# When TensorE's part of the gate tables is traced: at the step that makes its operands, or at the next weight

## The chip, the cores and the metric

The kernel runs on one core of a Trainium2 chip. The engines are TensorE (PE: matmuls, with PEld for its weight loads), VectorE (DVE), ScalarE (ACT), GpSimd (POOL, which issues the gathers here) and SyncE (SP, which issues the other DMAs). Each engine takes its instructions in a fixed order and waits where an operand or a buffer isn't ready. The metric is the time of one execution on the device in microseconds (us), as a median of several runs.

## What is computed

One block of a hybrid encoder over 1024 tokens of width 1024, in float32: a state space branch and a convolution branch, merged; then a mixer that looks up experts (PEER); then an embedding gate and a norm. The change touches the mixer alone:

```
scores = einsum("thcd,hckd->thck", q, keys)         # 8 heads, 2 halves, 128 keys each
sv, si = top_k(scores, 16)
best, j = top_k(all 16 x 16 sums of the two halves, 16)
expert = i1 * 128 + i2                              # one of 16384
gate = softmax(best)
act = gelu(einsum("thkd,td->thk", u_tab[expert], x))
out = einsum("thk,thkd->td", gate * act, v_tab[expert])
```

So each token has 8 x 16 = 128 chosen experts, each with a row of u_tab, a row of v_tab and a gate.

## The kernel before

The tokens are worked in two halves h of 512, each in four blocks b of 128. The mixer treats its blocks in two ways.

*Gathered blocks* (b of 0 and 1, four in all). `gather_up` fetches, for one choice of 128 tokens at a time, the rows of u_tab by an indirect DMA on POOL (L767) and multiplies and sums them with the tokens on DVE (L786). `gather_down` fetches rows of v_tab, four at a time, and PE adds them up with eight column-tiled matmuls ("gv", L814). All fetched rows lie in one ring of eight buffers, "row".

*Dense blocks* (b of 2 and 3). All 16384 experts are run: `dense_up(e)` takes the e-th 128 rows of u_tab, transposed (128 such blocks), as a weight, multiplies it with the 512 dense tokens and applies gelu. The result z goes to DRAM (DZ) or on to `dense_down`, which multiplies it by the table of gates (DG, zero where an expert wasn't chosen) and by v_tab's rows. One dense unit is 24 matmuls of 128x512, since every operand is split into a rounded part and a rest (`mm3`: L178, L179, L181).

`gate_table(i)` builds the table of one dense block i. First `choose_block` has found the choices; PE transposes them (L716) and ACT copies them to kt and wt. Then, for 4 tokens at a time (a *step*, 32 steps to a table in four chunks of eight), DVE makes the one-hot rows of both key numbers (L738) and puts the gates into the second (L740); PE multiplies the two (four products of 128x128, L744) and ACT copies the result to four tiles S (L747), which are written to DG at the end of a chunk (L750). The one-hots, too, lie in the "row" ring.

What sets the order: `weight()` loads a 128x1024 weight, splits it on ACT (L161) and DVE (L162), and then calls `tick`, which hands out work that lies beside the dense matmuls. Each tick adds a credit to three queues of generators (cq, gq, rq), and each is run until its yields have used the credit; a yield of None ends that turn. In the stage "up", gq holds a weave of the choices and tables (one after the other) with the gathers of u, one step of each in turn, and rq holds `gather_down`. What the generators trace is placed behind the tick's subtract (`issue_after`). A scheduler then fixes the order on each engine. Stage "up" runs dense units until gq is empty and the count is a multiple of four: 92 units. The rest of the 128 blocks come in "both" (up and down together, 36 blocks), and "down" then takes the 92 stored ones.

## Time and profile before

| | us |
|---|---|
| median of 3 runs | 4184.51 (4184.32 to 4186.64) |
| the profiled execution | 4184.43 |
| its span, first to last instruction | 4182.6 |
| stage "up" in the span | about 2020 to 2980 |
| stage "both" | about 2980 to 3394 |
| stage "down" | about 3394 to 4010 |

All times in the rows further below count from the start of the span. PE's busy time is that of pipelined matmuls; the granted clock is the share of 2.4 GHz that PE was given. A wait names the engine whose instruction could start only later, its line, what released it, the sum in us, how often, and the longest.

### The profile page before, as it was taken

Reading aid. Unit: us, or ns where it says so; the run is one execution under the profiler, and the core shown is the slowest. Engines: PE = TensorE matmul, PEld = TensorE weight load, DVE = VectorE, ACT = ScalarE, POOL = GpSimd, SP = SyncE. Lnnn points to the kernel's source line nnn. Section 1 sums busy time; section 2 is a strip of 40 time slices with the busy share of each in tenths; the row PEclk is TensorE's granted clock in tenths of the full one; section 3 lists DMA queues with packets and bytes.
Section 4 is the critical chain, followed back from the end, with each engine's and each line's share of the span. In section 5 each row is a group of like instructions: output and inputs, shape, how many; then the busy total and the mean of one; then the engine's idle time right before and its main releaser. Section 6 shows DMA issues by size and latency. Waiting matters only on the chain.

```text
span 4182.6 us, 51212 instructions
## 1 busy us (share of the span) xinstructions
PE 3783.2 (90%) x17800; PEld 2861.6 (68%) x17800; DVE 3121.7 (75%) x5907; ACT 1497.7 (36%) x2626; POOL 1283.1 (31%) x1087
## 2 busy tenths in 40 slices
PE   8999998899988897999879787888999999999987
PEld 6887776677866665667557565666777767777766
DVE  7889888989987876768978677677665656755545
ACT  4135565443345553433223232323322212222243
POOL 0000000000232433544655544454355444422000
PEclk9999998999999998999889898889999999999998
DMA  4243333453676878998989888888999999988632
GB/s 147 87 160 108 98 109 125 139 169 114 246 246 202 291 272 308 345 358 316 332 297 354 307 318 325 307 314 332 334 340 348 320 336 372 335 303 296 210 113 81
DMA packets 416068, 1057.77 MB, mean 253 GB/s; under 512 B 45184, under 2 KB 141568, under 8 KB 415808
## 3 DMA queue, kind: packets, MB, share of 16 engines
q1 hardware_dynamic: 268352, 517.56, 36.4%
q0 software_dynamic: 147456, 536.94, 35.6%
q8 instruction: 140, 2.29, 0.2%
q14 instruction: 120, 0.98, 0.1%
HBM read 953.01 MB, written 101.32 MB: 252 GB/s over the span
## 4 chain that ended last, share of the span: by engine, by line
PE 61%; DVE 14%; DMA 11%; issue 7%; ACT 4%; POOL 2%; SPq 1%; DVEq 0%; ACTq 0%; POOLq 0%
PE mm L178 11%; PE mm L179 11%; PE mm L181 10%; PE sp L178 7%; PE sp L179 6%; PE sp L181 6%; PE gv L814 4%; DMA row<-in_peer_u_dram,ix 3%; DVE row L786 3%; DVE hl L162 2%; DMA row<-in_peer_v_dram,ix 2%; POOL row L767 2%; PE sp L744 1%; DMA xr<-Dxt 1%; DMA A<-DZ 1%
## 5 line engine op out<-in xcount | busy, mean ns | idle before, releaser
L767 POOL DMA_INDIRECT row<-in_peer_u_dram,ix x512 | 628.2, 1227 | 1180.8 <-DMA ix<-Didx 446.2
L178 PE MATMUL mm<-xk,hl 128*128 128x512 f32 x2000 | 812.6, 411 | 73.5 <-ACT xk L169 30.3
L767 POOL DMA_INDIRECT row<-in_peer_v_dram,ix x512 | 647.8, 1265 | 752.8 <-PE gv L814 298.3
L179 PE MATMUL mm<-xk,hl 128*128 128x512 f32 x2000 | 804.3, 405 | 7.5 <-DVE xk L170 7.1
L786 DVE SCALAR_TENSOR_TENSOR row<-row,xr 128x1024 f32<-128x1024 f32 x512 | 617.1, 1222 | 232.5 <-DMA row<-in_peer_u_dram,ix 187.0
L161 ACT ACTIVATE hl<-raw 128x1024 fp32r<-128x1024 f32 x422 | 444.2, 1054 | 460.5 <-PE mm L181 313.0
L162 DVE TENSOR_TENSOR hl<-raw,hl 128x1024 fp32r<-128x1024 f32 x422 | 515.2, 1222 | 123.2 <-ACT hl L161 117.2
L181 PE MATMUL mm<-xk,hl 128*128 128x512 f32 x2000 | 515.1, 395 | 0.0
L178 PEld LDWEIGHTS mm<-xk,hl 128*128 128x128 f32 x2000 | 390.1, 196 | 180.6 <-ACT F L367 36.2
L179 PEld LDWEIGHTS mm<-xk,hl 128*128 128x128 f32 x2000 | 388.8, 195 | 104.6 <-DVE xk L170 14.8
L178 PE MATMUL sp<-xk,hl 128*128 128x512 f32 x1024 | 426.4, 417 | 5.6 <-ACT S L747 4.3
L181 PEld LDWEIGHTS mm<-xk,hl 128*128 128x128 f32 x2000 | 372.2, 188 | 85.5 <-issue 10.5
L179 PE MATMUL sp<-xk,hl 128*128 128x512 f32 x1024 | 416.9, 407 | 1.5 <-DVE xk L170 1.5
L314 DVE SCALAR_TENSOR_TENSOR ca<-cu,prm,ca 128x512 f32<-128x512 f32 x480 | 359.7, 749 | 34.9 <-ACT ca L312 26.8
L814 PE MATMUL gv<-row,sel 128*32 128x512 f32 x2048 | 292.7, 640 | 62.2 <-DMA row<-in_peer_v_dram,ix 56.9
L181 PE MATMUL sp<-xk,hl 128*128 128x512 f32 x1024 | 255.4, 390 | 0.0
L898 DVE TENSOR_TENSOR acc<-acc,sp 128x512 f32<-128x512 f32 x160 | 107.7, 685 | 197.0 <-PE sp L181 181.5
L178 PEld LDWEIGHTS sp<-xk,hl 128*128 128x128 f32 x1024 | 205.1, 200 | 67.1 <-issue 11.7
L744 PE MATMUL sp<-row 128*128 128x128 f32 x1024 | 152.6, 302 | 97.0 <-DVE row L740 87.5
L744 PEld LDWEIGHTS sp<-row 128*128 128x128 f32 x1024 | 140.5, 211 | 143.0 <-issue 104.9
L179 PEld LDWEIGHTS sp<-xk,hl 128*128 128x128 f32 x1024 | 203.7, 199 | 50.1 <-issue 5.9
L169 ACT ACTIVATE zs<-A 128x512 fp32r<-128x512 f32 x128 | 78.6, 622 | 416.5 <-PE sp L181 214.8
(267 smaller groups left out, 5840.7 us busy)
## 6 DMA issues: line engine op xcount, KB each, us to landing
raw<-in_w_in_dram SPq DMA_DIRECT2D x146, 512.0 KB
raw<-in_peer_ut_dram SPq DMA_DIRECT2D x128, 512.0 KB
raw<-in_peer_v_dram SPq DMA_DIRECT2D x128, 512.0 KB
DG<-S SPq DMA_DIRECT2D x64, 512.0 KB
G<-DG SPq DMA_DIRECT2D x128, 256.0 KB
DZ<-F SPq DMA_DIRECT2D x92, 256.0 KB
A<-DZ SPq DMA_DIRECT2D x92, 256.0 KB
ab<-Dac SPq DMA_DIRECT2D x32, 512.0 KB
```

Of the source, the lines that this page charges most:

```text
L161: nc.scalar.activation(h, raw, AF.Copy)
L162: self.tick(nc.vector.tensor_tensor(l, raw, h.bitcast(F32), op=OP.subtract))
L169: self.nc.scalar.activation(t[:, 0], src, AF.Copy)
L178: mm(ps, w[k][0], x[:, 0], start=start and k == 0, stop=False)
L179: mm(ps, w[k][0], x[:, 1], start=False, stop=False)
L181: self.pe = mm(ps, w[k][1], x[:, 0], start=False, stop=stop and k == n - 1)
L314: nc.vector.scalar_tensor_tensor(acc, u[:, j:j + 512], self.par("dw", i * 31 + j), acc, op0=OP.mult, op1=OP.add)
L744: nc.tensor.matmul(p[:, t * 128:(t + 1) * 128], oh[:, 0, t], oh[:, 1, t], start=True, stop=True)
L767: self.nc.gpsimd.indirect_dma_start(out=r, out_offset=None, in_=self.I[table], in_offset=bass.IndirectOffsetOnAxis(ap=ix[:, j, s:s + 1], a ...
L786: nc.vector.scalar_tensor_tensor(r, r, 1.0, xr, op0=OP.mult, op1=OP.mult, accum_out=act[:, j, s:s + 1])
L814: m = nc.tensor.matmul(po[32 * j:32 * j + 32, n, :], sel[:, j, s % 4, :], rows[j][:, n * 512:(n + 1) * 512], start=s == 0, stop=s == 31)
L898: nc.vector.tensor_tensor(self.acc[i], self.acc[i], p, op=OP.add)
```

## The change

The transposes of the choices and the products of a step are no longer traced where the choices or one-hots are made. They are put on a list, `later`, and the next `tick` traces them first, before it runs the queues. `gate_table` yields None while more than two entries wait on the list, so that a tick makes at most three steps, and it yields None until its kt and wt exist. The one-hots get a ring of their own with three buffers ("oh", 4 KB a partition), and F, the ring of the dense results, has 3 buffers in stage "up" instead of 8. The credit of gq in "up" is 7.8 instead of 7.2 a tick. The four tiles S are allocated when a chunk's first products are traced. No engine has more or fewer instructions than before, and stage "up" still has 92 units.

```diff
-                          choose1=(0, 0.8, 0.5), up=(0, 7.2, 0.5), both=(0, 1.5, 0.4), down=(0, 1.5, 0.4))
+                          choose1=(0, 0.8, 0.5), up=(0, 7.8, 0.5), both=(0, 1.5, 0.4), down=(0, 1.5, 0.4))
...
     def tick(self, anchor):
         with self.tc.issue_after(anchor.ins):
+            later, self.later = self.later, []
+            for f, a in later:
+                f(*a)
             self.cc = self.run(self.cq, self.cc + self.cr)
...
         if b >= HB:
-            p = self.sp()
-            for n, x in enumerate((ex[:, 128:256], ex[:, 0:128], gt[:])):
-                nc.tensor.transpose(p[:, n * 128:(n + 1) * 128], x, self.ident)
...
+            self.later.append((self.rows_of_choices, (HB * h + b - HB, ex, gt)))
...
     def gate_table(self, i):
-        db, kt, wt = next(t for t in self.tg if t[0] == i)
+        while i not in self.tg:
+            yield None
+        kt, wt = self.tg[i]
+
+        def products(c, q, oh):
+            if q == 0:
+                self.st = [self.A([128, 32, CT], tag="S") for _ in range(4)]
+            p = self.sp()
+            for t in range(4):
+                nc.tensor.matmul(p[:, t * 128:(t + 1) * 128], oh[:, 0, t], oh[:, 1, t], start=True, stop=True)
...
+                if q == CT // 4 - 1:
+                    nc.sync.dma_start(self.DG[i][:, c, n * 32:n * 32 + 32], s)
...
-                oh = self.row().rearrange("p (a t k) -> p a t k", a=2, t=4)
+                oh = self.scope.tile([128, 2, 4, 128], F32, name="oh", tag="oh", bufs=3)
...
+                self.later.append((products, (c, q, oh)))
+                while len(self.later) > 2:
+                    yield None
                 yield 1.9
...
         k.stage("up")
+        k.bufs.update(F=3)
...
-            while k.gq or e % k.G4:
+            while k.gq or k.later or e % k.G4:
```

The `rows_of_choices` on the list holds the transposes and copies that stood in `choose_block`, unchanged. From here on, lines of the changed kernel have other numbers: its products are L749, its one-hots L761 and L763, its u steps L803, its gv matmuls L831.

**Order 1**, in the second gate table. PE before, between two dense units: gv matmuls and two single steps of products.

```order
L814 MATMUL gv<-row,sel 32x512 x6
L744 MATMUL sp<-row 128x128 x4
L814 MATMUL gv<-row,sel 32x512 x2
L744 MATMUL sp<-row 128x128 x4
L178 MATMUL sp<-xk,hl 128x512
L179 MATMUL sp<-xk,hl 128x512
```

PE in the changed kernel, near the same place: the last part of a dense unit, and then the products of three steps.

```order
L183 MATMUL sp<-xk,hl 128x512
L185 MATMUL sp<-xk,hl 128x512 x8
L749 MATMUL sp<-oh 128x128 x12
L182 MATMUL sp<-xk,hl 128x512
L183 MATMUL sp<-xk,hl 128x512
L182 MATMUL sp<-xk,hl 128x512
```

Before, a step's four products stand alone among gv matmuls and units; now a tick's steps stand together in front of its dense unit. On DVE, the same table before, with one-hots (L738, L740), u steps (L786) and the subtract of a weight (L162):

```order
L738 TENSOR_TENSOR row<-io_84,kt 128x1024
L740 TENSOR_TENSOR row<-row,wt 128x512
L786 SCALAR_TENSOR_TENSOR row,act<-row,xr 128x1024
L740 TENSOR_TENSOR row<-row,wt 128x512
L786 SCALAR_TENSOR_TENSOR row,act<-row,xr 128x1024
L738 TENSOR_TENSOR row<-io_84,kt 128x1024
L740 TENSOR_TENSOR row<-row,wt 128x512
L738 TENSOR_TENSOR row<-io_84,kt 128x1024
L162 TENSOR_TENSOR hl<-raw,hl 128x1024
L740 TENSOR_TENSOR row<-row,wt 128x512
L738 TENSOR_TENSOR row<-io_84,kt 128x1024
L162 TENSOR_TENSOR hl<-raw,hl 128x1024
```

DVE in the changed kernel (L761 and L763 one-hots, L803 u steps, L166 the subtract):

```order
L761 TENSOR_TENSOR oh<-io_84,kt 128x1024
L803 SCALAR_TENSOR_TENSOR row,act<-row,xr 128x1024
L763 TENSOR_TENSOR oh<-oh,wt 128x512
L761 TENSOR_TENSOR oh<-io_84,kt 128x1024
L166 TENSOR_TENSOR hl<-raw,hl 128x1024
L761 TENSOR_TENSOR oh<-io_84,kt 128x1024
L763 TENSOR_TENSOR oh<-oh,wt 128x512 x2
L803 SCALAR_TENSOR_TENSOR row,act<-row,xr 128x1024
L761 TENSOR_TENSOR oh<-io_84,kt 128x1024
L166 TENSOR_TENSOR hl<-raw,hl 128x1024
L761 TENSOR_TENSOR oh<-io_84,kt 128x1024
L803 SCALAR_TENSOR_TENSOR row,act<-row,xr 128x1024
```

The pattern is the same; the one-hots now lie in their own ring, and their products wait for the next weight.

**Order 2**, POOL at the end of stage "up", where the last u rows of the third gathered block are fetched. Before, four rows of v_tab follow each few rows of u_tab:

```order
L767 DMA row<-in_peer_u_dram,ix 128x1024 x4
L767 DMA row<-in_peer_v_dram,ix 128x1024 x4
L767 DMA row<-in_peer_u_dram,ix 128x1024 x4
L767 DMA row<-in_peer_v_dram,ix 128x1024 x4
L767 DMA row<-in_peer_u_dram,ix 128x1024 x2
L767 DMA row<-in_peer_v_dram,ix 128x1024 x8
L767 DMA row<-in_peer_u_dram,ix 128x1024 x2
L767 DMA row<-in_peer_v_dram,ix 128x1024 x4
L767 DMA row<-in_peer_u_dram,ix 128x1024 x2
L767 DMA row<-in_peer_v_dram,ix 128x1024 x4
L767 DMA row<-in_peer_u_dram,ix 128x1024 x2
L767 DMA row<-in_peer_v_dram,ix 128x1024 x4
```

In the changed kernel, where the same u rows end, six groups of v rows follow in one piece:

```order
L784 DMA row<-in_peer_u_dram,ix 128x1024 x5
L784 DMA row<-in_peer_v_dram,ix 128x1024 x4
L784 DMA row<-in_peer_u_dram,ix 128x1024 x5
L784 DMA row<-in_peer_v_dram,ix 128x1024 x24
L784 DMA row<-in_peer_u_dram,ix 128x1024 x2
L784 DMA row<-in_peer_v_dram,ix 128x1024 x4
L784 DMA row<-in_peer_u_dram,ix 128x1024 x2
L784 DMA row<-in_peer_v_dram,ix 128x1024 x4
L784 DMA row<-in_peer_u_dram,ix 128x1024 x2
L784 DMA row<-in_peer_v_dram,ix 128x1024 x4
```

Fetches of v_tab have moved behind fetches of u_tab that they stood in front of; from the two u rows behind the piece on, the orders agree.

**Order 3**, the start of stage "up" on ACT. Before, the rounded parts of the eight loaded tiles (xk from F) stand together, in front of the first dense results:

```order
L790 ACTIVATE act<-act 128x4x16
L169 ACTIVATE xk<-F 128x512 x8
L870 ACTIVATE F<-sp 128x512
L161 ACTIVATE hl<-raw 128x1024
L870 ACTIVATE F<-sp 128x512
L161 ACTIVATE hl<-raw 128x1024
L870 ACTIVATE F<-sp 128x512
L161 ACTIVATE hl<-raw 128x1024
```

In the changed kernel the last two of the eight stand behind the Exp of the gates, L680:

```order
L807 ACTIVATE act<-act 128x4x16
L173 ACTIVATE xk<-F 128x512 x6
L680 ACT_TABLE_LOAD
L680 ACTIVATE gate<-gate 128x128
L173 ACTIVATE xk<-F 128x512 x2
L887 ACT_TABLE_LOAD
L887 ACTIVATE F<-sp 128x512
L165 ACTIVATE hl<-raw 128x1024
```

So the last two tiles of the dense operand come later in ACT's order.

## Rows read from the trace of the kernel before

**Rows 1.** The page's head: the span, and each engine's busy us (share of the span) and instructions.

```profile
span 4182.6 us, 51212 instructions
PE 3783.2 (90%) x17800; PEld 2861.6 (68%) x17800; DVE 3121.7 (75%) x5907; ACT 1497.7 (36%) x2626; POOL 1283.1 (31%) x1087
```

**Rows 2.** Windows of stage "up": from:to, length, then busy us (and instructions) of PE, PEld, DVE, ACT and POOL, the granted clock, the busy share of the DMA engines, and GB/s. The second, fourth, sixth and eighth row are the four gate tables, from the first one-hot to the last products; the rows between are the choosing stretches.

```profile
2020.00:2112.00 92.00, 76.94 (x356) 56.62 (x358) 87.33 (x255) 25.30 (x33) 57.33 (x40) 0.91 0.96 351
2112.00:2262.00 150.00, 129.09 (x683) 97.01 (x676) 111.18 (x162) 51.95 (x148) 77.89 (x58) 0.91 0.88 318
2262.00:2322.00 60.00, 50.70 (x242) 36.92 (x240) 48.39 (x123) 18.28 (x30) 30.10 (x22) 0.96 0.93 334
2322.00:2492.00 170.00, 139.48 (x697) 104.39 (x698) 116.33 (x174) 52.66 (x150) 87.11 (x67) 0.86 0.85 302
2492.00:2555.00 63.00, 46.06 (x220) 32.46 (x218) 45.22 (x117) 15.17 (x23) 32.04 (x29) 0.88 0.98 363
2555.00:2715.00 160.00, 130.92 (x675) 99.41 (x676) 112.47 (x167) 53.20 (x149) 74.07 (x58) 0.89 0.87 307
2715.00:2779.00 64.00, 54.62 (x255) 40.75 (x254) 49.43 (x120) 16.54 (x28) 32.76 (x26) 0.93 0.91 334
2779.00:2946.00 167.00, 135.94 (x714) 102.44 (x711) 122.50 (x206) 55.41 (x157) 86.09 (x66) 0.90 0.89 323
2946.00:2980.00 34.00, 34.00 (x165) 25.34 (x164) 21.56 (x56) 10.61 (x13) 4.13 (x5) 1.00 0.88 310
```

**Rows 3.** Waits from 2020 to 2980 us: who waited for whom, us in total, times, the longest.

```profile
DVE row L786 <- DMA row<-in_peer_u_dram,ix: 100.5, 52, 6.8
POOL row L767 <- PE sp L744: 96.1, 27, 12.2
PE sp L744 <- DVE row L740: 87.5, 28, 8.9
...
DVE row L738 <- PE sp L744: 58.8, 16, 9.9
ACT S L747 <- DMA DG<-S: 54.4, 32, 5.5
...
PE sp L716 <- DVE U L710: 27.1, 4, 15.1
```

**Rows 4.** PE's wait for the one-hots' last operation, the same columns, in each of the four tables (2112:2262, 2322:2492, 2555:2715, 2779:2946).

```profile
PE sp L744 <- DVE row L740: 3.9, 2, 3.6
...
PE sp L744 <- DVE row L740: 28.5, 8, 7.7
...
PE sp L744 <- DVE row L740: 32.8, 10, 8.9
...
PE sp L744 <- DVE row L740: 18.5, 7, 4.1
```

**Rows 5.** The queue of POOL's fetches (packets, MB, share of 16 engines), and sizes of DMAs with their counts.

```profile
q0 software_dynamic: 147456, 536.94, 35.6%
...
raw<-in_peer_ut_dram SPq DMA_DIRECT2D x128, 512.0 KB
...
DZ<-F SPq DMA_DIRECT2D x92, 256.0 KB
...
row<-in_peer_u_dram,ix POOLq DMA_INDIRECT x512
row<-in_peer_v_dram,ix POOLq DMA_INDIRECT x512
```

**Rows 6.** Windows of stage "both" and of the first half of "down", columns as in rows 2.

```profile
2980.00:3394.00 414.00, 412.20 (x1977) 308.81 (x1976) 248.34 (x344) 111.65 (x142) 214.44 (x177) 1.00 0.94 338
3394.00:3700.00 306.00, 287.70 (x1305) 215.81 (x1304) 203.06 (x297) 67.57 (x90) 126.87 (x104) 0.97 0.98 341
```

**Rows 7.** Timeline of PE: start, length, line, tiles and count, with instructions in a row merged. The rows are a group of gv matmuls, the ends of two dense units that follow each other with no other work between, and the products of two steps.

```profile
2056.99 1.92 PE L814 MATMUL gv<-row,sel 128*32 128x512 f32 x16
...
2081.09 1.98 PE L181 MATMUL sp<-xk,hl 128*128 128x512 f32 x8
...
2086.53 1.98 PE L181 MATMUL sp<-xk,hl 128*128 128x512 f32 x8
...
2621.59 1.95 PE L744 MATMUL sp<-row 128*128 128x128 f32 x16
```

**Rows 8.** The start of stage "up", 1950 to 2050 us: the loads of the eight tiles, their rounded parts on ACT and their rests on DVE (ns of one: shortest/median/longest, first and last start).

```profile
L862 SPq DMA_DIRECT2D F<-Dxd x8: 338/430/647, 2010.4 to 2013.9; - x8
...
L169 ACT ACTIVATE xk<-F x8: 629/630/632, 2015.6 to 2020.1; 128x512 fp32r<-128x512 f32 x8
L170 DVE TENSOR_TENSOR xk<-F,xk x8: 669/682/739, 2018.6 to 2027.4; 128x512 fp32r<-128x512 f32 x8
```

**Rows 9.** Groups of DVE instructions by line from 2000 to 2980 us: count | busy us, mean ns of one | idle us before them and what ended it.

```profile
L786 DVE SCALAR_TENSOR_TENSOR row<-row,xr 128x1024 f32<-128x1024 f32 x193 | 234.3, 1221 | 123.4 <-DMA row<-in_peer_u_dram,ix 100.5 <-DMA xr<-Dxt 18.3 <-issue 3.8
...
L738 DVE TENSOR_TENSOR row<-io,kt 128x1024 f32<-128x1024 bf16 x128 | 155.7, 1221 | 73.7 <-PE sp L744 58.8 <-PE gv L814 9.6 <-PE sp L181 3.2
...
L162 DVE TENSOR_TENSOR hl<-raw,hl 128x1024 fp32r<-128x1024 f32 x93 | 113.7, 1222 | 34.0 <-ACT hl L161 31.7 <-DMA raw<-in_peer_ut_dram 1.7 <-issue 0.5
...
L740 DVE TENSOR_TENSOR row<-row,wt 128x512 f32<-128x512 f32 x128 | 87.2, 687 | 1.1
```

More of the change, by code (lines that the diff above doesn't have):

```diff
@@ L78, in __init__ @@
         self.cc = self.gc = self.rc = 0.0
-        self.tg = []
+        self.tg = {}
+        self.later = []
         self.pend = []
@@ L712, in choose_block @@
         if b >= HB:
-            p = self.sp()
-            for n, x in enumerate((ex[:, 128:256], ex[:, 0:128], gt[:])):
-                nc.tensor.transpose(p[:, n * 128:(n + 1) * 128], x, self.ident)
-            kt = self.gp.tile([128, 2, 128], BF16, name="kt", tag="kt", bufs=4)
-            nc.scalar.activation(kt, p[:, 0:256].rearrange("p (a t) -> p a t", a=2), AF.Copy)
-            wt = self.gp.tile([128, 128], F32, name="wt", tag="wt", bufs=4)
-            nc.scalar.activation(wt, p[:, 256:384], AF.Copy)
-            self.tg.append((HB * h + b - HB, kt, wt))
+            self.later.append((self.rows_of_choices, (HB * h + b - HB, ex, gt)))
         else:
@@ L727, in choose_block, with rows_of_choices @@
             nc.sync.dma_start(self.Dgt[h][b], gt)
+    def rows_of_choices(self, i, ex, gt):
+        nc = self.nc
+        p = self.sp()
+        for n, x in enumerate((ex[:, 128:256], ex[:, 0:128], gt[:])):
+            nc.tensor.transpose(p[:, n * 128:(n + 1) * 128], x, self.ident)
+        kt = self.gp.tile([128, 2, 128], BF16, name="kt", tag="kt", bufs=4)
+        nc.scalar.activation(kt, p[:, 0:256].rearrange("p (a t) -> p a t", a=2), AF.Copy)
+        wt = self.gp.tile([128, 128], F32, name="wt", tag="wt", bufs=4)
+        nc.scalar.activation(wt, p[:, 256:384], AF.Copy)
+        self.tg[i] = kt, wt
     def gate_table(self, i):
         nc = self.nc
-        db, kt, wt = next(t for t in self.tg if t[0] == i)
+        while i not in self.tg:
[4 more added lines that the diff above has]
+                self.st = [self.A([128, 32, CT], tag="S") for _ in range(4)]
+            p = self.sp()
+            for t in range(4):
+                nc.tensor.matmul(p[:, t * 128:(t + 1) * 128], oh[:, 0, t], oh[:, 1, t], start=True, stop=True)
+            p4 = p.rearrange("p (t k) -> p t k", t=4)
+            for n, s in enumerate(self.st):
+                nc.scalar.activation(s[:, :, q * 4:q * 4 + 4].rearrange("p k t -> p t k"),
+                                     p4[:, :, n * 32:n * 32 + 32], AF.Copy)
+                if q == CT // 4 - 1:
+                    nc.sync.dma_start(self.DG[i][:, c, n * 32:n * 32 + 32], s)
         for c in range(NC):
-            st = [self.A([128, 32, CT], tag="S") for _ in range(4)]
             for q in range(CT // 4):
                 t0 = c * CT + q * 4
-                oh = self.row().rearrange("p (a t k) -> p a t k", a=2, t=4)
+                oh = self.scope.tile([128, 2, 4, 128], F32, name="oh", tag="oh", bufs=3)
                 nc.vector.tensor_tensor(oh, self.io128[:, None, None, :].to_broadcast([128, 2, 4, 128]),
@@ L740, in gate_table @@
                 nc.vector.tensor_tensor(oh[:, 1], oh[:, 1], wt[:, t0:t0 + 4, None].to_broadcast([128, 4, 128]), op=OP.mult)
+                self.later.append((products, (c, q, oh)))
+                while len(self.later) > 2:
+                    yield None
                 yield 1.9
-                p = self.sp()
-                for t in range(4):
-                    nc.tensor.matmul(p[:, t * 128:(t + 1) * 128], oh[:, 0, t], oh[:, 1, t], start=True, stop=True)
-                p4 = p.rearrange("p (t k) -> p t k", t=4)
-                for n in range(4):
-                    nc.scalar.activation(st[n][:, :, q * 4:q * 4 + 4].rearrange("p k t -> p t k"),
-                                         p4[:, :, n * 32:n * 32 + 32], AF.Copy)
-            for n in range(4):
-                nc.sync.dma_start(self.DG[db][:, c, n * 32:n * 32 + 32], st[n])
     def gather_setup(self, blk):
```

## The prediction

> **What bounds the kernel now.** First the page's busy shares [rows 1]: TensorE (PE) is busy 90% of 4182.6 us, so PE has about 400 us of idle time in all. Then the windows by stretch [rows 2], to find where that idle time lies. In the stage called "up" (2020 to 2980 us) four stretches build the gate tables: 150, 170, 160 and 167 us, 647 us together. There PE idles 20.9 + 30.5 + 29.1 + 31.1 = 112 us, at a granted clock of 0.86 to 0.91, a mean between full speed (2.4 GHz) and its lower level (1.2 GHz). The reader should see in the same rows that VectorE (DVE) is busy for 70 to 74% and the DMA engines for 85 to 89%, at 302 to 323 GB/s. The stretches between them (92, 60, 63, 64 and 34 us, 313 us together) are where choices are made; DVE (87 of 92 us in the first) and DMA (up to 363 GB/s) fill them. No engine is full in the tables: they wait for each other. The waits say how [rows 3]: PE waited 87.5 us for the one-hot rows that L740 finishes, while DVE waited 58.8 us at L738 for PE to give a ring slot back, and GpSimd (POOL) 96.1 us for the same slots before it could gather. One ring of eight "row" buffers serves the one-hots and the gathers, and PE meets a product as soon as DVE has made its operand [order 1]. By table, PE's wait at L744 was 3.9, 28.5, 32.8 and 18.5 us [rows 4].
>
> **What the change does to the order.** Counted down the PE order, the four tables now lie beside 13, 13, 13 and 11 dense units (24 matmuls each) instead of 14, 14, 14 and 13: 50 for 55. The stage keeps 92 units, so five units move to the choosing stretches. It also lets gathers fall behind: before unit 92 ends there are 37 groups of eight "gv" matmuls where there were 44 (24 instead of 30 of them inside the tables), and DVE has done 372 L786 steps there instead of 384. That is 28 v rows and 12 u rows, 40 fetches, that leave this stage and come back later [order 2]. One fetch moves 536.94 MB / 1024 = 0.524 MB, and a dense unit 512 + 256 KB = 0.786 MB [rows 5].
>
> **Tables.** They move 47.7 + 51.3 + 49.1 + 53.9 = 202 MB (time by GB/s of each row), on average 312 GB/s [rows 2]. Leaving: 24 v rows (12.6 MB) and 5 units (3.9 MB), so 185.5 MB stay. At what rate? Table 0 shows a table in which PE hardly waited for L740: 318 GB/s [rows 2, 4]. The upper row is the next stage, where the eight row buffers hold gathers alone, as they now will here: 338 GB/s [rows 6]. I take 325, nearer to table 0 since DVE still makes the same one-hots: 185.5 / 325 = 571 us, 76 less than 647. At 302 (the slowest table) it would be 614 (-33), at 338, 549 (-98). PE's own work is below all of these: 50 units at 5.44 us, 128 steps of four products at 0.98 us, 24 gv groups at 1.92 us [rows 7], together 444 us.
>
> The Trainium skill, "DMA: Bandwidth & Descriptors", section Specifications, puts HBM's share at about 358 GB/s per core. By that figure 185.5 MB can't take less than 518 us, an estimate, and the sum below would end at 4097 us at best; the trace has one stretch of 63 us at 363, so it agrees to about 1%.
>
> **Choosing stretches.** The transposes of L716 move to the next weight as well, and PE's 27.1 us of waiting there [rows 3] go. But DVE and DMA fill these stretches; 16 fewer fetches (8.4 MB) and 5 more units (3.9 MB) leave 4.5 MB less. I take -5 us, between -27 (PE's wait gone whole) and +12 (the five units cost their 3.9 MB at 334 GB/s).
>
> **F from 8 buffers to 3.** dense_in loads eight tiles through F. Now all eight loads are issued within 3.5 us, the first split starts 5.2 us after the first issue and the last ends at about 2028 [rows 8]. With three buffers they go in three rounds; each further round costs a flight of 5.2 us and a split of 0.63 + 0.68, so 13 us, and the last two splits stand behind the gate's Exp on ScalarE (ACT) [order 3]. DVE is full there with choices that it would do anyway [rows 2], so part is hidden: +8, between 0 and +20. For the dense results F is a ring of three units of over 10 us each (960 us / 92); a write to DZ needs one, so nothing.
>
> **Wider bursts.** PE now runs up to three steps of products in a row, and ACT copies them together. At the end of a chunk of eight steps the next chunk's first copy may follow directly, and then waits for the DG write: 12 inner boundaries at the longest wait of 5.5 us would be 66 us for the 54.4 there are [rows 3], +12 at most. Value 0: a dense unit of 5.44 us stands between most bursts and covers it. The list itself, the later allocation of the S tiles and the order of the 64 DG writes on SP's queue add no instruction.
>
> **What comes back.** In the next stage (36 expert blocks, each an up and a down unit of 24 matmuls, so up to unit 164) 29 gv groups stand for 26: 12 more fetches, 6.3 MB. PE is full there [rows 6], so at least 3 x 1.92 = 5.8 us; by DMA (139.9 + 6.3) MB / 341 = 429 us, +15. I take +9. Until the order is level again at unit 212, 17 groups stand for 13 and the 12 u rows come too: 28 fetches, 14.7 MB. That stretch has DMA at 0.98 and 341 GB/s [rows 6]: +43 if nothing hides it, 4 x 1.92 = +8 if only PE counts. I take +30, nearer to the full DMA. Behind it the two orders agree.
>
> **Sum.** -76 - 5 + 8 + 0 + 9 + 30 = -34 us. The profiled execution took 4184.4 us (1.8 us around its span), the median of the runs 4184.5, so no correction: 4150 us.
>
> **Rivals.**
> *DMA runs full in the tables* (chance 0.15). If the freed row buffers let the tables reach the 363 GB/s of the best choosing stretch, they take 511 us (-136), and the sum is 4184 - 136 + 42 = 4090, where 42 is all that stands beside the tables. For it: POOL's 96.1 us of waiting for one-hot slots. Against: DVE still waited 100.5 us for u rows [rows 3], and no table passed 323.
> *A loop between DVE and PE* (0.18), slower. The one-hot ring has three buffers, and a unit now makes 2.56 steps (128 / 50). DVE can't make the next ones until PE has run the last ones, which stand behind a whole dense unit, and PE reaches the next burst with DVE unfinished [order 1]. Then one period holds, end to end, 2.56 x (1.221 + 0.687) us of one-hots, 2.56 x 1.221 of u steps woven between, 1.22 of L162 [rows 9], 2.56 x 0.98 of products [rows 7] and DVE's 100.5 / 92 = 1.1 of waiting for gathers [rows 3]: 12.8 us. Fifty of them are 641 us, and the sum is 4184 - 6 + 42 = 4220. It decides from 12.1 us a unit, where the tables take 605. For it: DVE's 58.8 us at L738 are this loop in small, and with 3.9 us of PE wait table 0 still took 150 us. Against: DVE may start on the slots as the first step of a burst ends, and L162 with two or three u steps can be done meanwhile.
> *The wait is passed on* (0.12). L744 no longer waits, but PE waits as long for v rows or ring slots; the tables stay at about 306 GB/s (606 us, -41) and what comes back eats it: 4185.
>
> **How the numbers follow.** The forecast (0.55) covers tables at 312 to 338 GB/s, 4128 to 4174. A measurement of this kernel can tell about 0.2%, 8.4 us, from no change. Faster: 0.53 of the forecast and 0.15, 0.68. Same: 0.11 of the passed-on wait and some of each neighbour, 0.14. Slower: 0.18. The range of 8 in 10, 4095 to 4200, leaves out most of the loop (0.14) and the best of the full DMA (0.06).
>
> **What would show it.** PE's wait at the products for DVE falls from 87.5 us to under 30; the tables take 545 to 600 us with DMA at 0.90 or more; POOL no longer waits for one-hot slots; the stretch from the end of unit 164 to unit 212 grows by 8 to 43 us, and the one before it by 6 to 15. PE's first unit of "up" ends up to 20 us later. I am wrong if DVE's wait for the oh ring grows past 90 us (the loop), if the tables stay above 600 us, or if what comes back costs nothing, in which case the gain is near 70.

## The result and the profile after

| | us |
|---|---|
| median of the kernel before | 4184.41 (4180.44 to 4186.64, 4 runs) |
| median of the changed kernel | 4083.93 (4076.53 to 4089.80, 4 runs) |
| ratio | 0.976, 95% interval 0.9738 to 0.9782 |
| the profiled execution after | 4076.53 |

The change takes 100 us off the kernel, three times the 34 us forecast, and the time lies below the range's lower end of 4095. The page's head of the changed kernel, with the columns of [rows 1]:

```profile
span 4074.7 us, 51241 instructions
...
PE 3740.6 (92%) x17800; PEld 2835.8 (70%) x17800; DVE 3116.5 (76%) x5907; ACT 1490.9 (37%) x2626; POOL 1291.3 (32%) x1087
```

PE's busy time itself is 42.6 us less than in [rows 1], though it runs the same 17800 matmuls. (The 29 instructions more in the head are of kinds that no engine's busy time counts; the five engines have the same counts as before.) Windows of "up", of "both" and of the first 48 units of "down", columns as in [rows 2]; here the borders are PE's own: tables run from their first to their last product, stages end with PE's last unit. The second, fourth, sixth and eighth row of the first block are the tables; the second block has "both" and the 48 units of before, for comparison.

```profile
2016.00:2140.00 124.00, 96.52 (x428) 65.02 (x421) 108.43 (x293) 30.02 (x42) 67.93 (x54) 0.85 0.89 322
2140.00:2269.00 129.00, 117.81 (x665) 93.18 (x666) 108.81 (x167) 52.60 (x152) 76.83 (x55) 0.96 0.97 360
2269.00:2318.00 49.00, 48.32 (x229) 36.77 (x227) 43.33 (x110) 15.88 (x27) 25.73 (x20) 1.00 1.01 376
2318.00:2446.00 128.00, 117.64 (x666) 92.86 (x667) 106.58 (x164) 52.39 (x151) 73.17 (x50) 0.97 0.95 344
2446.00:2494.00 48.00, 48.00 (x230) 36.90 (x229) 44.18 (x109) 15.81 (x27) 26.95 (x22) 1.00 1.01 389
2494.00:2618.00 124.00, 116.83 (x666) 92.40 (x665) 105.38 (x162) 52.46 (x152) 66.74 (x50) 0.97 0.97 356
2618.00:2666.00 48.00, 47.46 (x225) 36.40 (x224) 42.28 (x105) 15.79 (x26) 25.14 (x20) 1.00 1.01 374
2666.00:2799.00 133.00, 111.00 (x626) 87.78 (x625) 109.69 (x180) 50.36 (x146) 77.76 (x54) 0.90 0.95 352
2799.00:2829.00 30.00, 30.00 (x142) 23.36 (x141) 28.22 (x80) 10.44 (x20) 17.41 (x13) 1.00 1.02 373
2829.00:3291.00 462.00, 454.37 (x2184) 336.04 (x2182) 258.65 (x359) 114.06 (x148) 224.27 (x193) 0.99 0.96 343
3291.00:3637.00 346.00, 313.01 (x1442) 227.96 (x1442) 230.78 (x338) 75.57 (x101) 157.52 (x131) 0.96 0.99 350
```

```profile
2973.00:3429.30 456.30, 448.69 (x2140) 335.34 (x2143) 262.10 (x366) 116.41 (x149) 223.68 (x186) 0.99 0.94 334
3429.30:3742.30 313.00, 300.51 (x1378) 225.41 (x1378) 210.84 (x305) 73.53 (x99) 126.25 (x103) 0.98 0.97 341
```

On PE, then, "both" of the kernel before ends at 3429.3 us (unit 164), 35 us behind the 3394 of the table of stages and of [rows 6].

No table is below 344 GB/s, where those of [rows 2] had 302 to 323. The choosing stretches show PE full and up to 389 GB/s. Cut in the same way, the trace of before and that of after compare as follows (us):

| stretch | before | after | difference | forecast |
|---|---|---|---|---|
| start of "up" to the first product | to 2115.2 | to 2139.8 | +24.6 | +8 |
| four tables | 153.3 + 172.4 + 168.9 + 161.2 = 655.8 | 129.3 + 127.8 + 123.9 + 133.0 = 514.0 | -141.8 | -76 |
| three choosing stretches between | 172.6 | 145.5 | -27.1 | -5 |
| end of "up" (unit 92) | 2973.0 | 2828.9 | -144.1 | |
| "both" | 456.3 | 462.3 | +6.0 | +9 |
| 48 units of "down" | 313.0 | 345.8 | +32.8 | +30 |
| the rest to the end | 440.3 | 437.7 | -2.6 | 0 |

The last four rows make the 107.9 us between the two spans (4182.6 and 4074.7; the execution profiled after is the fastest of its four). What came back later is 38.8 us where 39 was forecast, so the error of the sum lies in front of unit 92. Each trace is a single execution, though. The stage's first load is issued at 2010.4 us before and at 2012.6 after, and between 2002.7 and 2018.1 in the traces of the kernels below, so a time of one trace that counts from the start of the span carries some us that the edit did not make.

The waits in "up" of the changed kernel, columns as in [rows 3]:

```profile
POOL row L784 <- PE gv L831: 144.7, 27, 13.4
...
DVE oh L761 <- PE sp L749: 54.6, 24, 5.4
...
ACT S L752 <- DMA DG<-S: 31.9, 20, 6.3
...
DVE row L803 <- DMA row<-in_peer_u_dram,ix: 30.6, 18, 5.9
PE gv L831 <- DMA row<-in_peer_v_dram,ix: 28.8, 7, 16.6
PE sp L749 <- ACT S L752: 28.7, 8, 8.3
...
PE sp L182 <- ACT S L752: 9.8, 3, 5.1
...
PE sp L749 <- DVE oh L763: 7.4, 6, 3.6
```

PE's wait for the one-hots fell from 87.5 us to 7.4, DVE's for u rows from 100.5 to 30.6, and POOL hardly waits for products any more (2.1 us for 96.1). Its longest wait is for gv matmuls, which give back slots with v rows in them; that was so before too (the window of [rows 3]),

```profile
POOL row L767 <- PE gv L814: 110.4, 29, 10.2
```

and this wait has grown in the shorter stage. DVE waits nearly as long for one-hot slots as it did (54.6 for 58.8), now in its own ring. What is new is that PE waits for ACT's copies into the tiles S, 28.7 us at the products and 9.8 at dense matmuls, where before it was 5.7 and 4.3; ACT itself waits 31.9 us there for tiles S whose write to DG hasn't ended.

Two views tell what the sum of waits doesn't. The first is the window of the whole stage, of before and then of after:

```profile
2016.00:2973.00 957.00, 792.98 (x3957) 592.30 (x3958) 716.75 (x1384) 301.43 (x733) 484.62 (x368) 0.90 0.90 323
```

```profile
2016.00:2829.00 813.00, 733.59 (x3862) 564.67 (x3855) 696.90 (x1361) 295.75 (x732) 457.67 (x332) 0.95 0.96 354
```

PE's idle time fell from 164.0 to 79.4 us, but its busy time fell too, from 793.0 to 733.6, and the granted clock rose from 0.90 to 0.95. The second view is PE's groups by line over the same stretches (count | busy us, mean ns of one | idle before them). Before:

```profile
L178 PE MATMUL sp<-xk,hl 128*128 128x512 f32 x737 | 313.6, 426 | 5.6 <-ACT S L747 4.3 <-ACT xk L169 1.2
...
L744 PE MATMUL sp<-row 128*128 128x128 f32 x1024 | 152.6, 302 | 97.0 <-DVE row L740 87.5 <-ACT S L747 5.7 <-DVE hl L162 1.3
L814 PE MATMUL gv<-row,sel 128*32 128x512 f32 x704 | 110.1, 683 | 32.6 <-DMA row<-in_peer_v_dram,ix 32.6
```

After:

```profile
L182 PE MATMUL sp<-xk,hl 128*128 128x512 f32 x737 | 302.6, 412 | 11.8 <-ACT S L752 9.8 <-ACT xk L173 2.0
...
L749 PE MATMUL sp<-oh 128*128 128x128 f32 x1024 | 135.8, 285 | 37.5 <-ACT S L752 28.7 <-DVE oh L763 7.4 <-ACT F L887 1.4
L831 PE MATMUL gv<-row,sel 128*32 128x512 f32 x608 | 79.1, 626 | 28.8 <-DMA row<-in_peer_v_dram,ix 28.8
```

The rows have two records for each gv matmul and each product (1024 for the 512 products). 96 gv records (six groups) have left the stage, at 79.1 / 608 = 0.13 us some 12.5 us. The other 47 us of busy time are of the same instructions, which are shorter now: a gv record takes 626 ns for 683, a product's 285 for 302, a dense matmul of L178 (now L182) 412 for 426. Most of that is the clock. The granted clock is a mean of two levels, 1.2 and 2.4 GHz. In the windows above it is 1.00 where PE was full (the choosing stretches) and 0.90 in the table with the most idle time (111.00 of 133.00 us busy). In the clock records of the two traces, PE falls to the lower level 25 times in "up" before, for 184 us, and 11 times after, for 85 us, and each fall comes behind idle time of PE. With each stretch of PE's busy time weighted by its granted clock, the 793.0 and 733.5 us become 728.1 and 707.1: 38 of the 59 us are the clock, some 12 the matmuls that left, and the rest isn't explained. So a wait is paid for a second time, in the matmuls that run at the lower level.

### The profile page after: what moved, and what is told of

The parts are those of the page before. It is cut to its first block, busy times and chain, and to the rows that moved or that the text cites. A ratio compares the mean times of both kernels' runs of the same rounds, so it can differ in the third digit from the quotient of the medians.

```text
span 4074.7 us, 51241 instructions
## 1 busy us (share of the span) xinstructions
PE 3740.6 (92%) x17800; PEld 2835.8 (70%) x17800; DVE 3116.5 (76%) x5907; ACT 1490.9 (37%) x2626; POOL 1291.3 (32%) x1087
## 5 line engine op out<-in xcount | busy, mean ns | idle before, releaser
L784 POOL DMA_INDIRECT row<-in_peer_u_dram,ix x512 | 645.5, 1261 | 1083.7 <-DMA ix<-Didx 418.5
L182 PE MATMUL mm<-xk,hl 128*128 128x512 f32 x2000 | 814.5, 412 | 72.9 <-ACT F L371 30.7
L784 POOL DMA_INDIRECT row<-in_peer_v_dram,ix x512 | 638.7, 1247 | 733.5 <-DVE row L803 314.4
L803 DVE SCALAR_TENSOR_TENSOR row<-row,xr 128x1024 f32<-128x1024 f32 x512 | 614.7, 1221 | 167.7 <-DMA row<-in_peer_u_dram,ix 134.2
L166 DVE TENSOR_TENSOR hl<-raw,hl 128x1024 fp32r<-128x1024 f32 x422 | 514.7, 1221 | 108.6 <-ACT hl L165 107.6
L182 PEld LDWEIGHTS mm<-xk,hl 128*128 128x128 f32 x2000 | 391.1, 196 | 181.0 <-ACT F L371 38.2
L182 PE MATMUL sp<-xk,hl 128*128 128x512 f32 x1024 | 415.4, 407 | 11.8 <-ACT S L752 9.8
L183 PE MATMUL sp<-xk,hl 128*128 128x512 f32 x1024 | 409.5, 401 | 6.4 <-DVE xk L174 6.4
L831 PE MATMUL gv<-row,sel 128*32 128x512 f32 x2048 | 267.0, 613 | 42.7 <-DMA row<-in_peer_v_dram,ix 37.3
L185 PE MATMUL sp<-xk,hl 128*128 128x512 f32 x1024 | 256.9, 391 | 0.0
L182 PEld LDWEIGHTS sp<-xk,hl 128*128 128x128 f32 x1024 | 198.2, 194 | 69.9 <-ACT S L752 12.0
L915 DVE TENSOR_TENSOR acc<-acc,sp 128x512 f32<-128x512 f32 x160 | 107.7, 685 | 172.6 <-PE sp L185 172.6
L183 PEld LDWEIGHTS sp<-xk,hl 128*128 128x128 f32 x1024 | 198.4, 194 | 55.5 <-issue 7.5
L185 PEld LDWEIGHTS sp<-xk,hl 128*128 128x128 f32 x1024 | 191.5, 188 | 49.1 <-issue 9.2
L182 PE MATMUL sp<-zs,vhl 128*128 128x512 f32 x480 | 186.7, 401 | 19.6 <-DVE acc L915 19.6
```

The lines of the kernel that those rows point to most:

```text
L166: self.tick(nc.vector.tensor_tensor(l, raw, h.bitcast(F32), op=OP.subtract))
L182: mm(ps, w[k][0], x[:, 0], start=start and k == 0, stop=False)
L183: mm(ps, w[k][0], x[:, 1], start=False, stop=False)
L185: self.pe = mm(ps, w[k][1], x[:, 0], start=False, stop=stop and k == n - 1)
L784: self.nc.gpsimd.indirect_dma_start(out=r, out_offset=None, in_=self.I[table], in_offset=bass.IndirectOffsetOnAxis(ap=ix[:, j, s:s + 1], a ...
L803: nc.vector.scalar_tensor_tensor(r, r, 1.0, xr, op0=OP.mult, op1=OP.mult, accum_out=act[:, j, s:s + 1])
```

## The experiments

Each edit is of the kernel before or of the changed kernel ("after"). The ratio is to runs of the kernel before on the same chip, with its 95% interval. The columns behind it are read from the profiled execution as in the table above: units in "up", then us of the tables, of the choosing stretches, the end of "up", the length of "both" and of "down", and for "up" as a whole PE's idle time, the granted clock, MB and GB/s.

| kernel | median us | ratio | units | tables | choosing | end of up | both | down | PE idle | clock | MB | GB/s |
|---|---|---|---|---|---|---|---|---|---|---|---|---|
| before | 4184.41 | 1 | 92 | 655.8 | 172.6 | 2973.0 | 456.3 | 584.6 | 164.0 | 0.90 | 309 | 323 |
| after | 4083.93 | 0.9760 | 92 | 514.0 | 145.5 | 2828.9 | 462.3 | 615.5 | 79.4 | 0.95 | 288 | 354 |
| ring_only | 4094.62 | 0.9792 [0.9769, 0.9815] | 92 | 542.6 | 142.3 | 2838.5 | 464.6 | 616.0 | 83.5 | 0.95 | 288 | 350 |
| list_only | 4183.05 | 0.9995 [0.9982, 1.0008] | 92 | 628.5 | 196.3 | 2975.6 | 453.9 | 598.7 | 182.0 | 0.90 | 309 | 322 |
| f3_only | 4195.37 | 1.0019 [1.0005, 1.0034] | 92 | 658.4 | 164.3 | 2970.0 | 456.2 | 595.2 | 173.1 | 0.91 | 307 | 322 |
| after_S | 4082.61 | 0.9760 [0.9737, 0.9782] | 92 | 524.1 | 144.4 | 2813.6 | 469.1 | 627.0 | 76.3 | 0.95 | 279 | 349 |
| after_dz2 | 4098.97 | 0.9810 [0.9782, 0.9838] | 92 | 527.7 | 144.4 | 2826.0 | 463.2 | 636.3 | 90.5 | 0.95 | 297 | 367 |
| before_dz2 | 4204.35 | 1.0055 [1.0035, 1.0074] | 92 | 666.9 | 178.9 | 2987.2 | 446.6 | 592.7 | 180.7 | 0.90 | 333 | 343 |
| before_r78 | 4223.09 | 1.0114 [1.0083, 1.0146] | 88 | 634.0 | 173.9 | 2968.3 | 512.4 | 562.6 | 195.2 | 0.89 | 301 | 316 |
| ring_r78 | 4138.67 | 0.9894 [0.9878, 0.9911] | 88 | 562.6 | 142.5 | 2886.0 | 510.0 | 575.5 | 130.7 | 0.91 | 298 | 342 |
| list_r72 | 4221.15 | 1.0082 [1.0059, 1.0105] | 100 | 686.4 | 193.5 | 3039.7 | 352.9 | 664.3 | 181.7 | 0.90 | 324 | 316 |
| after_r72 | 4069.28 | 0.9733 [0.9708, 0.9759] | 100 | 522.4 | 147.2 | 2841.0 | 368.6 | 689.5 | 54.0 | 0.96 | 290 | 352 |
| after_r66 | 4072.42 | 0.9736 [0.9720, 0.9753] | 104 | 540.7 | 148.0 | 2870.0 | 311.7 | 721.8 | 56.8 | 0.97 | 294 | 345 |
| ring2 | 4146.24 | 0.9912 [0.9892, 0.9932] | 92 | 619.9 | 138.1 | 2919.2 | 455.5 | 598.9 | 133.9 | 0.91 | 306 | 339 |
| before_rr42 | 4142.20 | 0.9886 [0.9847, 0.9925] | 92 | 617.9 | 151.9 | 2919.8 | 452.4 | 596.6 | 144.4 | 0.91 | 295 | 327 |
| ring_rr6 | 4115.08 | 0.9822 [0.9804, 0.9840] | 92 | 571.0 | 141.6 | 2880.9 | 462.3 | 608.7 | 106.3 | 0.93 | 296 | 343 |
| after_nomul | 4070.45 | 0.9725 [0.9694, 0.9755] | 92 | 521.6 | 144.0 | 2824.3 | 460.8 | 606.9 | 79.7 | 0.94 | 286 | 354 |

### Which part brings the gain: the ring, the list, or F

*ring_only*: before, with the ring of its own and F of 3; products stay in place and the credit is 7.2.

```diff
-                oh = self.row().rearrange("p (a t k) -> p a t k", a=2, t=4)
+                oh = self.scope.tile([128, 2, 4, 128], F32, name="oh", tag="oh", bufs=3)
...
+        k.bufs.update(F=3)
```

> The kernel before, with the one-hots in their own ring of three and F at 3 (to make room), but every product still traced behind its one-hots and 7.2 as the credit. Ring theory (the row buffers given back to the gathers keep the DMA engines full): the four tables, 656 us from first to last product of each before and 514 in the changed kernel, fall to 560 or less, DMA at 0.94 or more, and over half of the 100 us is here. List theory (PE's wait for L740 set the pace): tables stay above 620, PE still waits 70 us or more at the products. If both parts are needed: tables 580 to 620.

*list_only*: after, with the same two edits turned back; list and credit 7.8 stay.

> The changed kernel with its one-hots back in the row ring of eight and F at 8; products and transposes still traced at the next weight, credit 7.8. List theory: tables at 560 us or less, over half of the 100 us. Ring theory: the one-hots now hold row buffers for a whole unit, POOL waits for products as long as before (96 us) or longer, tables above 620 and a total within 1% of the kernel before, perhaps slower. Order counts: the gv groups before the end of unit 92 stay at 44, so nothing comes back later and the two later stages should keep their lengths.

*f3_only*: before, with `k.bufs.update(F=3)` alone.

> The kernel before with F at 3 buffers in stage up and nothing else. It measures the price of the small F ring alone: the first product comes 25 us later in the changed kernel (2140 for 2115 us). If that delay lies on the path, 4195 to 4210; if the full DVE and DMA of the first stretch hide it, 4180 to 4190. DZ writes should cost nothing.

The ring alone gives 0.9792, 87 us; the list with the row ring gives nothing, and F alone costs 8 us (2 to 14). The waits in "up" of ring_only:

```profile
DVE oh L738 <- PE sp L744: 75.8, 31, 7.9
...
DVE row L786 <- DMA row<-in_peer_u_dram,ix: 28.9, 24, 2.4
...
PE sp L744 <- DVE oh L740: 11.2, 6, 8.1
```

and of list_only:

```profile
DVE row L803 <- DMA row<-in_peer_u_dram,ix: 114.3, 44, 9.2
...
PE sp L749 <- DVE row L763: 62.9, 18, 7.2
POOL row L784 <- PE sp L749: 55.3, 29, 6.3
```

With products traced in place, PE's wait for the one-hots still falls from 87.5 to 11.2 us. It was no matter of PE meeting a product too early. With the list but without the ring PE waits 62.9 us, and POOL 55.3 for the products to give slots back. So the wait began at the shared slots: POOL could not fetch until products had run, u rows came late, DVE waited for them in front of its one-hots, and PE for DVE. How much of the 87 us is this and how much is gathers that the order hands out later is the question of "Slots or later gathers" below.

### The start of the stage

*after_S*: after, with the eight loads through four idle S tiles instead of three F buffers.

```diff
-        self.dx = [self.split(self.zt(self.Dxd[k], "F")) for k in range(KT)]
+        ts = [self.A([128, 2, 512], tag="S") for _ in range(KT // 2)]
+        for k in range(KT):
+            self.nc.sync.dma_start(ts[k // 2][:, k % 2], self.Dxd[k])
+        self.dx = [self.split(ts[k // 2][:, k % 2]) for k in range(KT)]
```

> The changed kernel with the eight tiles of dense_in loaded into the four S tiles (free until the first table), two in each, so that they no longer go through the F ring in three rounds. If the late start is on the path: the first product 15 to 25 us earlier and the total 10 to 25 us less, 4060 to 4075. If DVE and DMA set the pace of the first stretch, within 8 us of 4084.

The start in the changed kernel (columns as in [rows 8]):

```profile
L879 SPq DMA_DIRECT2D F<-Dxd x8: 319/320/424, 2012.6 to 2033.4; - x8
L173 ACT ACTIVATE xk<-F x8: 616/630/633, 2017.1 to 2042.9; 128x512 fp32r<-128x512 f32 x8
L174 DVE TENSOR_TENSOR xk<-F,xk x8: 672/680/693, 2020.8 to 2043.6; 128x512 fp32r<-128x512 f32 x8
```

The loads are issued over 20.8 us instead of 3.5 [rows 8], and the last rest on DVE starts at 2043.6 instead of 2027.4. PE's fourth unit ends at 2058.6 for 2045.0. In after_S that unit ends at 2035.9 and the first product at 2115.7, 24 us earlier than after's, of which 9.6 us are an earlier first load (2003.0 for 2012.6). Yet the time is the same: tables, "both" and "down" take 28 us more. The stage ends earlier, and less of the gathering (279 MB for 288) lies beside it. Counted from the first load, f3_only shows what the three rounds do alone: the fourth unit ends 8.6 us later than before (43.2 for 34.6) and the first product comes 9.9 us later. Its 8 us in the total fit that in size, but where they arise isn't shown: its "up" is 4.3 us longer from the first load on, its "down" 10.6.

### Is the DMA rate the limit

*after_dz2* and *before_dz2*: each dense result is written to DRAM twice, 92 x 0.262 = 24.1 MB more in "up", and nothing else.

```diff
-                nc.sync.dma_start(k.DZ[e], k.dense_up(e))
+                z = k.dense_up(e)
+                nc.sync.dma_start(k.DZ[e], z)
+                nc.sync.dma_start(k.DY[e], z)
```

> The changed kernel with every dense result of stage up written to DRAM twice (92 writes of 0.262 MB more, 24.1 MB; nothing reads the copies). If the DMA engines set the pace of the tables and choosing stretches now, stage up grows by 24.1 MB / 361 GB/s = 67 us, 55 to 75 with what the order moves. If PE or DVE sets it, under 15 us.

> The kernel before with the same second write. If its tables were held by waits between engines and not by DMA, their slack (DMA at 0.85 to 0.89) takes most of the 14 MB that fall into them, and stage up grows by 10 to 35 us. If DMA set the pace before as well, by 24.1 MB / 325 GB/s = 74 us.

"Up" as a whole in after_dz2:

```profile
2016.00:2826.00 810.00, 719.55 (x3779) 560.52 (x3780) 676.93 (x1313) 294.71 (x729) 418.68 (x305) 0.95 0.97 367
```

and its four tables:

```profile
2124.00:2258.00 134.00, 119.63 (x667) 93.82 (x667) 107.75 (x169) 52.23 (x150) 73.27 (x54) 0.95 0.97 365
2306.00:2431.00 125.00, 114.55 (x649) 91.67 (x649) 104.36 (x159) 52.61 (x151) 65.91 (x48) 0.97 0.99 368
2479.00:2619.00 140.00, 120.22 (x669) 94.81 (x668) 112.22 (x179) 54.16 (x154) 80.22 (x57) 0.93 0.97 365
2667.00:2796.00 129.00, 107.31 (x607) 86.51 (x608) 108.69 (x194) 50.64 (x146) 63.43 (x45) 0.91 0.96 359
```

Stage "up" did not end later (2826.0 for 2828.9), and 367 GB/s were moved in it; 297 MB are there and not 312, since 4 gv groups and some u rows fell behind and came back in "down", 21 us longer. So 354 GB/s was no ceiling, and the 338 of [rows 6] still less. More than that the run doesn't show. The tables took 527.7 us for 514.0 with some 11 MB more in them, and the stage ends no later only because it began earlier (first load at 2002.7 for 2012.6, first product at 2124.3 for 2139.8). Their 359 to 368 GB/s are 1 to 7% above those of the changed kernel's tables, at a DMA share of 0.96 to 0.99: how near to the limit of DMA the changed kernel's tables run stays open. In before_dz2 the whole 24 MB went into the stage (333 MB for 309) and it ended 14.2 us later, inside the 10 to 35 us expected if waits held it, and far from the 74 us of a full DMA. The Trainium skill, "DMA: Bandwidth & Descriptors", section Specifications, gives about 358 GB/s a core, on which the forecast worked out 4097 us at best; "HBM Reference", section Specifications (TRN2), says that a core which streams alone goes well above that share. The runs side with the second: 367 over 810 us, and 374 to 389 in the choosing stretches above.

### What the credit does

The credit alone: 7.8 in the kernel before (*before_r78*) and in ring_only (*ring_r78*), 7.2 in list_only (*list_r72*) and in after (*after_r72*), 6.6 in after (*after_r66*).

```diff
-                          choose1=(0, 0.8, 0.5), up=(0, 7.8, 0.5), both=(0, 1.5, 0.4), down=(0, 1.5, 0.4))
+                          choose1=(0, 0.8, 0.5), up=(0, 7.2, 0.5), both=(0, 1.5, 0.4), down=(0, 1.5, 0.4))
```

> The kernel before with the credit of gq in stage up at 7.8 instead of 7.2 and nothing else. Stage up then has 88 units and both has 40 blocks. If the credit alone mattered, up to 20 us faster; I expect within 0.5% of 4184, since the work is the same and DMA and the waits set the pace, with four units less to write to DZ and read back (2 x 1.05 MB, 6 us).

> The ring alone (products traced in place, F at 3) with the credit of 7.8: 88 units in up. If the credit costs by the units that it takes out of up, four units at some 8 us each: 4120 to 4135. If the credit only cost because of the shared ring, 4085 to 4105.

> The list with one-hots in the row ring and F at 8, now with the old credit of 7.2: stage up then has 100 units (92 before, 88 in the kernel before with 7.8). The credit of 7.8 alone cost the kernel before 40 us, so the list at 7.8 may have hidden a gain of its own. If so, 4135 to 4160; if the list alone is worth nothing, 4175 to 4195.

> The changed kernel with the old credit of 7.2. Stage up then has 100 units and both 28 blocks; more gathers come back later (34 gv groups before unit 92). If DMA is full in up, the eight more units there cost 8 x 0.786 MB in up and their DZ reads later: 4085 to 4115. If the credit of 7.8 is what made the gain, 4140 or more.

> The changed kernel with a credit of 6.6: 104 units in up and 24 blocks in both. At 7.2 (100 units) it took 4069, 15 us less than at 7.8 (92 units), since units in up fill idle PE time. Four more: 4055 to 4070 if they still come nearly free, 4070 to 4085 if PE or DMA is full by now or the gathers that fall behind cost as much.

Four of the five came out beside what was expected of them; after_r66 came by its second case. The credit sets how many units stand beside the tables, and 7.8 costs against 7.2: 48 us in the kernel before, 43 with the ring, 11 in the changed kernel, where the intervals still overlap (ratios times 4184). Before_r78 shows why: four units fewer end "up" only 4.7 us earlier, because they had filled time in which PE waited, but "both" grows by 56.1 and "down" shrinks by 22.0. With the ring and the list 100 units are best or near it: PE's idle time in "up" falls to 54.0 us, and **after_r72 has the lowest median of all, 4069.28 us**, though its interval overlaps the changed kernel's. The list is worth little by itself: at 92 units 13 us with the ring (after against ring_only, intervals overlapping) and nothing without it (list_only against before). At an equal credit it adds units to the stage, which is good with the ring (25 us at 7.2, ring_only against after_r72; 56 us at 7.8, ring_r78 against after) and, at 7.2 with the row ring, bad (list_r72, 34 us slower than before).

### Slots or later gathers

Ring_only also hands out less gathering beside "up" (39 gv groups by unit 92 for 44, and 368 u steps for 384), so 21 MB leave the stage. Three kernels part the two. *ring2* has the ring with two buffers, and its order hardly lags (42 and 384). *before_rr42* has no ring, but the rate of `gather_down` in "up" is 0.42 for 0.5 (37 and 384). *ring_rr6* is ring_only with that rate at 0.6 (43 and 365).

```diff
-                          choose1=(0, 0.8, 0.5), up=(0, 7.2, 0.5), both=(0, 1.5, 0.4), down=(0, 1.5, 0.4))
+                          choose1=(0, 0.8, 0.5), up=(0, 7.2, 0.42), both=(0, 1.5, 0.4), down=(0, 1.5, 0.4))
```

> The ring alone with two buffers instead of three. In its order the gathers hardly fall behind: 42 gv groups before the end of unit 92 (44 before, 39 with three buffers) and all 384 u steps. Slot theory (the row ring left to the gathers keeps DMA full): tables at 590 us or less in sum, total 4090 to 4125. Lag theory (up got short because 40 fetches left it): up ends above 2920 and the total is above 4150.

> The kernel before with the rate at which the down gathers are handed out in up lowered from 0.5 to 0.42, nothing else: by unit 92 the order holds 37 down gathers where it held 44 (the changed kernel holds about 37), still 92 units in up, one-hot rows still in the row ring. If the gain of the own ring comes from the order handing out the down gathers later (some 7 groups of 2.6 MB, 18 MB less in up), up ends near 2900 us or earlier and the time is 4095 to 4145 us. If it comes from the row slots that the one-hot rows no longer hold, up ends within 25 us of 2973, the wait of PE for the gate multiply (L740) stays above 60 us, and the time is 4165 to 4200 us.

> The kernel before with the one-hot ring alone (ring_only), and the rate of the down gathers in up raised from 0.5 to 0.6, so that by unit 92 the order holds 43 of them, nearly the 44 of the kernel before, where ring_only holds 39. If the slots give the gain, PE's wait for L740 stays under 25 us, the tables sum to 530 to 570 us and the time is 4085 to 4115 us. If the later gathers give it, the tables come back to over 600 us and the time is 4140 us or more.

Neither explanation holds alone, and ring2 fell between its two forecasts. Later gathers without the ring give 48 us (interval 31 to 64), at hardly more GB/s (327 for 323): the stage is shorter by the bytes that left it. The slots with hardly any lag give 37 us (28 to 45), at nearly the same bytes and 339 GB/s. Together they make 85 us, and ring_only has 87; ring_rr6, with the three slots and about 13 MB of the lag, lies between at 74. The waits in "up" fit: before_rr42 keeps most of them,

```profile
POOL row L767 <- PE sp L744: 95.1, 33, 6.7
...
PE sp L744 <- DVE row L740: 67.1, 20, 7.0
```

and ring2 more than halves PE's:

```profile
PE sp L744 <- DVE oh L740: 30.7, 12, 6.4
```

Two buffers are one less than the change has, so the split is no exact one.

### What sets the pace now

*after_nomul*: after, without the multiply by the gates in `gate_table`. The output lacks the gates of the dense blocks; 128 x 0.69 = 88 us of DVE's work are gone.

```diff
-                nc.vector.tensor_tensor(oh[:, 1], oh[:, 1], wt[:, t0:t0 + 4, None].to_broadcast([128, 4, 128]), op=OP.mult)
```

> The changed kernel without the multiply of the one-hot rows by the gates (L763), 128 instructions of some 0.69 us on VectorE, 88 us of its work; the output lacks the gates of the lower half. If VectorE sets the pace of the tables now (it is busy 109 of 129 us in one), their sum falls from 514 to 470 us or less and the time to 4050 us or less. If the DMA rate or TensorE sets it, the sum stays between 500 and 520 and the time between 4070 and 4090 us.

```profile
2016.00:2824.00 808.00, 728.30 (x3836) 562.40 (x3836) 615.92 (x1210) 294.72 (x729) 425.74 (x327) 0.94 0.96 354
```

```profile
DVE oh L761 <- PE sp L749: 87.6, 33, 6.8
```

These are "up" as a whole and DVE's wait for the one-hot ring. DVE does 81 us less in the stage, and the tables take no less (521.6 for 514.0); the time is 13 us lower with overlapping intervals. DVE spends what it saved waiting for PE to give one-hot slots back (87.6 us for 54.6). So DVE's work does not hold the tables. PE is busy for 90% of "up", and the credit shows how much room it has left: eight units more (after_r72) lengthen the stage by 12.1 us, where eight take 8 x 5.44 = 43.5 us of PE [rows 7], and four more (after_r66) by another 29.0, about what they and the three more gv groups there take (21.8 + 5.8). So at 92 units PE still has idle time that units can fill, and at 100 hardly any. Of the 79.4 us that it idles in the changed kernel, 38.5 are waits for the copies into S; in after_r72 these are 19.0 of 54.0. Whether the order on PE, the four tiles S or, by the open end of after_dz2, the DMA rate holds the tables at 92 units isn't shown: no run made PE's work less or gave S more buffers.

## Why the prediction was wrong, point by point

- **What bounds the stage** was read rightly in the tables: no engine full, one ring for one-hots and gathers, POOL's 96.1 us for slots. (DVE's share there is 68 to 74% in [rows 2], not 70 to 74.) But the text put the change's weight on PE meeting its operand; the runs put it on the slots and on the gathers that leave.
- **The tables' rate is the step that failed.** "I take 325", between 302 and 338. The bytes were nearly right (181.4 MB measured, 185.5 forecast), the rate was 353, so the tables took 514 us and not 571, and the step of dividing the bytes by a rate read from other stretches gave -76 where the runs gave -141.8. In its place the runs show that the rate followed from who holds the ring's slots: one more ring took it up (ring_only, 350 GB/s in "up" for 323), later gathers alone hardly (before_rr42, 327). The 338 of [rows 6] was taken as what DMA can do. There PE is full (412.20 of 414.00 us), so those rows show what PE's work asks for, and no ceiling. The 363 and 351 GB/s in [rows 2] spoke against it and were left to a rival.
- **PE's own work** was set at 444 us by the durations of [rows 7], all at the full clock. [rows 2] had 535 us of PE's busy time in the same stretches; after, the four tables have 463. Of the difference between 535 and 444, the five units and six groups that leave make 5 x 5.44 + 6 x 1.92 = 39 us, and the rest is the lower clock that the waits bring: weighted by its granted clock the 535 us are 482. The sum had no term for busy time that goes when the waits go.
- **Choosing stretches**: -5 forecast, -27.1 measured, the bound named there. The reason given, that DVE and DMA fill them, fell: in the three between the tables DVE was busy for only 72 to 81% [rows 2], DMA went from 334 to 363 GB/s up to 374 to 389, and PE is now full.
- **F**: the mechanism was right (three rounds), the last rest 16.2 us later and PE's unit 4 by 13.6, of which 2.2 us are the later first load, for +8 forecast. Alone it costs 8 us (f3_only); that it costs anything in the changed kernel is not shown, since after_S takes it away and the time stays.
- **Wider bursts**: value 0. PE waited 28.7 us at the products for S's copies where before it was 5.7, and 9.8 for 4.3 at dense matmuls. The reason for 0, that a dense unit between the bursts covers it, didn't hold; what the wait costs in the end isn't shown.
- **What comes back**: +39 forecast, +38.8 measured. The count of fetches by the order was right, and DMA is full in the first half of "down" (0.99 now), but that the sizes agree this well is in part luck. The forecast worked with the border at 3394, where PE's is 3429.3. "Both" and the 48 units together took 780.9, 779.8 and 767.7 us in list_only, f3_only and before_dz2, whose order brings nothing back, for 769.3 in before, a spread of 13 us without any cause in the fetches; and in before_rr42, with as many gv groups coming back as in the changed kernel but hardly any u rows, they took 778.0, only 8.7 us more than in before.
- **Rivals.** The full DMA came nearest in size (4090, from 363 GB/s in the tables, where 353 came). That 353 is no ceiling after_dz2 shows; how far below one it lies stays open, so this rival is neither shown nor ruled out. The loop between DVE and PE did not come: DVE waited 54.6 us for the oh ring, under the 90 given. Most of the wait was not passed on: PE's idle time fell by 84.6 us, and its wait for v rows from 32.6 to 28.8; only its wait for S's copies grew.
- **The credit** was counted only through the 92 units that stay. Set back to 7.2 it gives 100 units and about 11 us more gain, which is not clear of the noise.

## What to carry to other kernels

A wait's named engine may itself be starved through a ring that it shares with the waiter: find who holds the slots before moving the waiting instruction. GB/s of a stretch in which another engine is full may be that engine's demand; before it is taken for a ceiling, look for a faster stretch or add bytes. When idle time of TensorE goes, price its busy time too, at the clock that the stretch would then have.

## What the hardware showed that was not expected

- One core moved 367 GB/s over 810 us (after_dz2) and 389 over 48 us (after), beside matmuls.
- The clock pays waits twice: with 85 us less PE idle time in "up", the same matmuls took some 47 us less, 38 of them by the granted clock (0.95 for 0.90).
- A unit taken from "up" saved 1.2 us there in the kernel before (4.7 / 4) and cost 8.5 later ((56.1 - 22.0) / 4), by one trace of each kernel.
